# Tiles of the large products allocated on multiples of 256 bytes in a two-block fp32 transformer kernel

## The chip, the cores and the metric

The kernel runs on one core of a Trainium2 chip. The metric is the time of one execution in device microseconds (us). TensorE (PE) multiplies, VectorE (DVE), ScalarE (ACT) and GpSimd (POOL) do the rest, SyncE (SP) issues the transfers from HBM. In one product a *moving* operand streams through the array while a *stationary* operand sits in it; the stationary operand is loaded by a separate operation, which the profile lists as the engine PEld.

## The reference, cut to what matters

Two transformer blocks in a row on 256 tokens of 2048 features, all in fp32:

```
x   = x + norm(mixer(norm(x)) @ w_out)             # three branches: two attentions and an RWKV recurrence
x   = x + norm(square(relu(norm(x) @ w_mlp_up)) @ w_mlp_down)        # 8192 wide
x   = x + concat(pool, latent attention, memory attention) @ w_o
x   = x + (silu(conv(n @ w_gate)) * (n @ w_up)) @ w_down             # 5632 wide, n = norm(x)
```

Nearly all the arithmetic is in the products with the weight matrices: `w_in` (2048 x 12580, with the three gates), `w_out`, `w_mlp_up`, `w_mlp_down`, `w_gate`, `w_up`, `w_down` and smaller ones. The attentions, the recurrence and the norms are small beside them.

## The kernel before, in words

**A number in two parts.** TensorE works on the type fp32r. To keep fp32 accuracy each factor is held as a sum of two fp32r tiles, `hi` and `lo`; a product is `hi*hi + hi*lo + lo*hi`, added up in PSUM. Activations are split once (`split`), into tiles of shape [128, k, 2, 256]: for each slice k of 128 features 256 columns of the high part and then 256 of the low part. Their names in the trace are `uhl` (input of block 1), `yaT`, `ybT`, `ychl` (branches), `mhl` (the mix), `memhl` (memory), `A` (input of the MLP, then of block 2), `B` (hidden layer of the MLP, a group at a time), `kvhl`, `qhl` (latents), `catT`, `x3hl` (input of the last layers) and `h2`, shown as `h` (its hidden layer).

**A unit of weights.** `load` brings 512 KB of weights as [128, 1024] fp32 into `raw` (three buffers) with one transfer issued by SP, ACT copies it to `hi` (three buffers), and DVE writes `lo = raw - hi` (three buffers). All nine buffers are 4096 bytes long in each partition.

**Two kinds of product.** `lin_t` gives the result feature-major: the weights are stationary (128 columns at a time) and the activations move. For every slice of weights it does a *pair*: `hi` against 512 moving columns (both parts of the activations) and `lo` against 256 (the high part). `lin_n` gives the result token-major: the activations are stationary and the weights move, 512 columns at a time (384 for `w_q_up`, 320 for one piece of block 2's `w_in`), three matmuls for a slice: activations high on `hi`, high on `lo`, low on `hi`. So in the trace `m<-uhl,hi` names the moving tile first in `lin_t`, and `m<-hi,B` names the moving weights first and the stationary tile `B` second in `lin_n`. `m` is the PSUM bank; `s` stands for the banks of all small products.

**Order.** A scheduler orders the instructions at build time, and pools decide each tile's address. The splits in `load` have a raised priority, so a unit's `hi` and `lo` are made as soon as its buffers are free. Where a tile asks for nothing, the pools put it on the next multiple of 32 bytes. Every matmul of both kinds goes through the helper at L159, every ACT instruction through L178, every DVE `tensor_tensor` through L166.

**Order of the work in time.** The mixer (`uhl` moving, with the attentions and the recurrence between) to about 890 us, `w_out` (`mhl`) to 981, half of the memory product (`memhl`), four groups of the MLP (`A` moving, then `B` stationary) to 1723, the other half of the memory product, block 2's input product (`A` stationary) to 1836, its attentions to about 1890, `w_o` (`catT`), then three groups of `x3hl` moving and `h` stationary to the end.

Of the kernel before, what the change touches and what calls it, by code (L numbers as in the profile page):

```python
# [10 lines left out]
F32 = mybir.dt.float32  # L11
F32R = mybir.dt.float32r
# [3 lines left out]
PSUM = bass.MemoryType.PSUM  # L16
# [15 lines left out]
NB = 16  # L32

# [90 lines left out]
class K:  # L124
# [78 lines left out]
    def split(self, hl, src, scale=None):  # L203
        """hl: [128, 2, n] F32R; src fp32 (SBUF or PSUM); hl[0] + hl[1] == src * scale."""
        hi, lo = hl[:, 0], hl[:, 1]
        if scale is None:
            self.act(hi, src, AF.Copy)
            self.tt(lo, src, hi.bitcast(F32), ALU.subtract)
        else:
            self.act(hi, src, AF.Identity, scale=scale)  # L210
            self.stt(lo, src, scale, hi.bitcast(F32), ALU.mult, ALU.subtract)

    def load(self, parts, kt, nc_):
        """parts: (column, DRAM rows [kt*128, n]); the weights of one unit, split."""
# [71 lines left out]
    def halves(self, out, ps, m=P, lo=0):  # L286
        """out = the sum of a bank's halves."""
# [4 lines left out]
    def bcast_rows(self, r):  # L292
        """r [128 tok, 2] -> PSUM [128, 256] with r along the free axis on all partitions."""
# [5 lines left out]
    def sum_features(self, acc):  # L299
        """acc [128 feat, 256] -> PSUM [128 tok, 2] of sums over the partitions."""  # L300
# [33 lines left out]
    # decay and in-context rate  # L334
# [11 lines left out]
    # 1 / max(|kk|, 1e-12) by token, chunk and head  # L346
# [20 lines left out]
def rwkv_pair(k, tl, j, zr, zk, zv, sg, aa, rin, omka, col, gu1, gu2, sg1, sg2, yc):  # L367
    """Two heads (128 features); two chunks of 128 tokens."""
    C = k.C
    # features of the recurrence  # L370
# [40 lines left out]
    # token-major copies  # L411
# [12 lines left out]
    # scores, [s, t]; i = 2 * chunk + head  # L424
# [11 lines left out]
    # inverse of I + L: its transpose's blocks of 16 on the diagonal by substitution, each row by itself  # L436
    # (the block's entries, from DRAM, on all of its rows)
# [25 lines left out]
    # doubling of the blocks, here of 16: only every other n columns change  # L463
# [32 lines left out]
    # right-hand sides, solution, outputs, state  # L496
# [36 lines left out]
    # bonus and gate  # L533
# [10 lines left out]
    def finish():  # L544
        # norm by head, gain
# [52 lines left out]
def softmax_tile(k, tl, z, n, p, first=True):  # L598
    """p = softmax over the free axis of z [128, n]."""
# [44 lines left out]
def causal_out(k, tl, z, v, out):  # L644
    """z [128, 384]: scores of queries 0..127 (128 keys) and 128..255 (256 keys)."""
# [14 lines left out]
def mixer(k, a, xhl):  # L660
    """-> mg: mix * norm_mix_post, feature-major, and its factor by token."""
# [38 lines left out]
    yaT = tl([P, 4, 2, 256], "yaT", F32R)  # L700
    ybT = tl([P, 4, 2, 256], "ybT", F32R)
# [54 lines left out]
    # gates and branches  # L756
# [47 lines left out]
def post_stats(k, pool, acc, z, j, n):  # L804
    """acc += z * z (feature-major)."""
# [9 lines left out]
def block_kernel(ctx, tc, vecs, rows, cst1, cst2, out, **a):  # L815
# [19 lines left out]
    xhl = tl(up, [P, 16, 2, 256], "uhl", F32R)  # L835
# [27 lines left out]
    # residual stream, feature-major  # L863
# [4 lines left out]
    # memory: normed and transposed; its keys and values fill the turns between phases  # L868
# [6 lines left out]
    memhl = tl(memp, [P, 16, 2, 256], "memhl", F32R)  # L875
# [67 lines left out]
    # MLP  # L943
# [4 lines left out]
    for g in range(G):  # L948
        h = tl(pB, [P, KG, 2, 256], "B", F32R)
# [24 lines left out]
    def r_mlp(r, ss, t):  # L974
        # y carries no 1/rms of its input yet: y_true = r1^2 y
# [7 lines left out]
    x2hl = tl(pA, [P, 16, 2, 256], "A", F32R)  # L983
# [7 lines left out]
def block2(k, main, pA, a, rows, cst2, x2hl, rz, xres, mk, mv, out):  # L991
# [10 lines left out]
    # projections of the normed input  # L1002
# [40 lines left out]
    def unit_heads(nm_, z):  # L1043
        """The memory attention's queries and keys, over their norms by head."""
# [26 lines left out]
    kvhl = lp.tile([P, 2, 2, 256], F32R, tag="kvhl", name="kvhl")  # L1071
    qhl = lp.tile([P, 4, 2, 256], F32R, tag="qhl", name="qhl")
# [12 lines left out]
    catT = pA.tile([P, 16, 2, 256], F32R, tag="A", name="catT")  # L1085
    # pooling
# [16 lines left out]
    # memory attention  # L1103
# [25 lines left out]
    # keys and values  # L1129
# [19 lines left out]
    # queries; their factors by token join the scores  # L1149
# [18 lines left out]
    # latent attention by pairs of heads  # L1168
# [27 lines left out]
    # output product; x3 and its norm  # L1196
# [11 lines left out]
    x3hl = pB.tile([P, 16, 2, 256], F32R, tag="B", name="x3hl")  # L1208
# [16 lines left out]
    # token-major residual  # L1225
# [11 lines left out]
    for gi, (n0, nn) in enumerate(groups):  # L1237
        h = pA.tile([P, 16, 2, 256], F32R, tag="A", name=k.nm("h2"))
# [73 lines left out]
```

## Time and profile before

| | us |
|---|---|
| runs | 2766.87, 2770.70, 2780.21 (median 2770.7) |
| span of the profiled execution | 2761.2 |
| PE busy | 2691.8 (97%) |
| PEld busy | 2261.6 (82%) |
| DVE busy | 1735.1 (63%) |
| ACT busy | 1391.4 (50%) |
| DMA engines, by their packets | 54% of the span |

The span runs from the first to the last instruction of the program in one profiled execution; a run's time also holds what lies around it. The median run is 9.5 us longer than this span, and the runs themselves lie 13 us apart. The profiled execution's own time is not listed apart from its span. A busy PE is not a PE at its peak: a matmul's row in the trace counts from its start to the modelled end of its last column, and rows overlap, so how fast matmuls follow one another is read from the distance between their starts.

### The profile page before, as it was taken

The numbers are of one execution on the slowest core, as the hardware profiler recorded it, in microseconds if no ns is written. First come the engines' busy times: TensorE is split into PE (matmuls) and PEld (weight loads), VectorE is DVE, ScalarE is ACT, GpSimd is POOL, SyncE is SP. The second block draws the span as 40 slices with busy tenths as digits, with TensorE's granted clock in tenths as the row PEclk, the third lists the DMA queues.
The fourth block names the chain that finished last, engine by engine and source line by source line (L and its number), as shares of the span: only waits on it lengthen the run. The fifth ranks groups of instructions, "written<-read, shape, count | busy, mean of one in ns | idle before, by whom it ended". The sixth has DMA issues, their size and how long they took to land.

```text
span 2761.2 us, 38434 instructions
## 1 busy us (share of the span) xinstructions
PE 2691.8 (97%) x14588; PEld 2261.6 (82%) x14588; DVE 1735.1 (63%) x2985; ACT 1391.4 (50%) x2245; POOL 37.1 (1%) x36
## 2 busy tenths in 40 slices
PE   7999999999999999999999999999999999999999
PEld 6777787877888888888888888878788888888887
DVE  6657576567666566455565565757767567647764
ACT  7445364454555665444344444666655445535543
POOL 0000000000000000000000000000000000000000
PEclk9999999999999999999999999999999999999999
DMA  6444344454456756565565655544456556555555
GB/s 186 131 133 140 109 133 130 147 156 130 151 185 211 257 171 189 187 190 190 189 190 187 189 191 189 173 154 135 136 164 189 188 186 190 185 189 188 186 189 177
DMA packets 390232, 475.69 MB, mean 172 GB/s; under 512 B 20112, under 2 KB 306832, under 8 KB 390048
## 3 DMA queue, kind: packets, MB, share of 16 engines
q1 hardware_dynamic: 390016, 473.18, 54.2%
q8 instruction: 114, 1.87, 0.3%
q14 instruction: 70, 0.57, 0.1%
q0 software_dynamic: 32, 0.07, 0.0%
HBM read 470.82 MB, written 2.36 MB: 171 GB/s over the span
## 4 chain that ended last, share of the span: by engine, by line
PE 83%; issue 5%; DVE 5%; DMA 3%; ACT 1%; POOL 0%; POOLq 0%; SPq 0%; DVEq 0%; ACTq 0%
PE m L159 77%; PE s L159 5%; DMA mb<-md 3%; DVE lo L166 2%; PE s L163 1%; DVE zw L166 1%; DVE zc L166 1%; ACT hi L178 1%; DVE SM L166 0%; DVE Z L166 0%; POOL rs L195 0%; DVE zz L166 0%; DMA raw<-in_w_in 0%; DVE xres L169 0%; POOL qrs L195 0%
## 5 line engine op out<-in xcount | busy, mean ns | idle before, releaser
L166 DVE TENSOR_TENSOR lo<-raw,hi 128x1024 fp32r<-128x1024 f32 (+1 forms) x874 | 1063.2, 1217 | 768.6 <-ACT hi L178 765.2
L178 ACT ACTIVATE hi<-raw 128x1024 fp32r<-128x1024 f32 (+1 forms) x874 | 920.1, 1053 | 1051.3 <-PE m L159 799.5
L159 PE MATMUL m<-uhl,hi 128*128 128x512 f32 (+1 forms) x1456 | 528.7, 403 | 2.4 <-DVE zz L166 2.4
L159 PE MATMUL m<-x3hl,hi 128*128 128x512 f32 x1408 | 494.6, 394 | 0.0
L159 PE MATMUL m<-uhl,lo 128*128 128x256 f32 (+1 forms) x1456 | 419.2, 288 | 13.5 <-DVE lo L166 13.5
L159 PE MATMUL m<-x3hl,lo 128*128 128x256 f32 x1408 | 398.3, 283 | 0.0
L159 PE MATMUL m<-A,hi 128*128 128x512 f32 x1024 | 356.0, 393 | 1.8 <-DVE A L169 1.8
L159 PEld LDWEIGHTS m<-uhl,hi 128*128 128x128 f32 (+1 forms) x1456 | 275.6, 189 | 67.0 <-DVE zz L166 3.3
L159 PE MATMUL m<-hi,B 128*128 128x512 f32 x1024 | 321.6, 395 | 0.0
L159 PEld LDWEIGHTS m<-x3hl,hi 128*128 128x128 f32 x1408 | 264.4, 188 | 61.0
L159 PEld LDWEIGHTS m<-uhl,lo 128*128 128x128 f32 (+1 forms) x1456 | 277.1, 190 | 17.6 <-DVE lo L166 15.2
L159 PE MATMUL m<-A,lo 128*128 128x256 f32 x1024 | 286.7, 281 | 0.0
L159 PEld LDWEIGHTS m<-x3hl,lo 128*128 128x128 f32 x1408 | 264.7, 188 | 0.1
L159 PEld LDWEIGHTS m<-hi,B 128*128 128x128 f32 x1024 | 192.9, 188 | 45.0
L159 PEld LDWEIGHTS m<-A,hi 128*128 128x128 f32 x1024 | 191.8, 188 | 44.8 <-DVE A L169 2.4
L159 PE MATMUL m<-hi,h 128*128 128x512 f32 x704 | 221.7, 395 | 0.0
L159 PE MATMUL m<-lo,B 128*128 128x512 f32 x512 | 202.0, 395 | 0.0
L159 PEld LDWEIGHTS m<-A,lo 128*128 128x128 f32 x1024 | 192.5, 188 | 0.8 <-DVE lo L166 0.3
L159 PEld LDWEIGHTS m<-hi,h 128*128 128x128 f32 x704 | 131.9, 187 | 32.4
L178 ACT ACTIVATE hv<-m 128x256 f32<-128x256 f32 x323 | 120.0, 374 | 55.1 <-PE m L159 53.5
L159 PE MATMUL m<-lo,h 128*128 128x512 f32 x352 | 139.1, 395 | 0.0
L166 DVE TENSOR_TENSOR zz<-m,hv 128x256 f32<-128x256 f32 x307 | 126.9, 418 | 17.7 <-ACT hv L178 17.7
(373 smaller groups left out, 3014.6 us busy)
## 6 DMA issues: line engine op xcount, KB each, us to landing
raw<-in_w_in SPq DMA_DIRECT2D x220, 512.0 KB, 3.5
raw<-in_w_mlp_up SPq DMA_DIRECT2D x128, 512.0 KB, 3.8
raw<-in_w_mlp_down SPq DMA_DIRECT2D x128, 512.0 KB, 3.4
raw<-in_w_gate SPq DMA_DIRECT2D x88, 512.0 KB, 3.5
raw<-in_w_up SPq DMA_DIRECT2D x88, 512.0 KB, 3.6
raw<-in_w_down SPq DMA_DIRECT2D x88, 512.0 KB, 3.5
raw<-in_w_out SPq DMA_DIRECT2D x32, 512.0 KB, 4.6
raw<-in_w_o SPq DMA_DIRECT2D x32, 512.0 KB, 3.6
```

What stands on the lines that cost most here:

```text
L159: self.pe.matmul(out, lhsT=lhsT, rhs=rhs, start=start, stop=stop)
L163: self.pe.transpose(out, in_, self.C["ident"][:n, :n])
L166: self.v.tensor_tensor(out=out, in0=a, in1=b, op=op)
L178: self.a.activation(out, in_, f, **k)
```

## The change

Seventeen allocations ask for a start on a multiple of 256 bytes: the three tiles of `load` (`raw`, `hi`, `lo`, three buffers each) and all split activations. Nothing else is changed in the program text but that comments are blank lines now, and that the new constant moves each later line down by one (L159 is L160 in the changed kernel).

```diff
 NB = 16
+LINE = 256
@@ load
-        raw = self.wr.tile([P, 1024], F32, tag="raw", name=self.nm("raw"))
-        hi = self.wh.tile([P, 1024], F32R, tag="hi", name=self.nm("hi"))
-        lo = self.wl.tile([P, 1024], F32R, tag="lo", name=self.nm("lo"))
+        raw = self.wr.tile([P, 1024], F32, tag="raw", name=self.nm("raw"), align_bytes=LINE)
+        hi = self.wh.tile([P, 1024], F32R, tag="hi", name=self.nm("hi"), align_bytes=LINE)
+        lo = self.wl.tile([P, 1024], F32R, tag="lo", name=self.nm("lo"), align_bytes=LINE)
@@ block_kernel
-    xhl = tl(up, [P, 16, 2, 256], "uhl", F32R)
+    xhl = tl(up, [P, 16, 2, 256], "uhl", F32R, align_bytes=LINE)
...
-        h = tl(pB, [P, KG, 2, 256], "B", F32R)
+        h = tl(pB, [P, KG, 2, 256], "B", F32R, align_bytes=LINE)
...
-    x3hl = pB.tile([P, 16, 2, 256], F32R, tag="B", name="x3hl")
+    x3hl = pB.tile([P, 16, 2, 256], F32R, tag="B", name="x3hl", align_bytes=LINE)
```

Likewise `yaT`, `ybT`, `mhl`, `ychl`, `memhl`, the three tiles in the place `A` (`act_hl`, `x2hl`, `catT`), `kvhl`, `qhl` and `h2`. The addresses that the pools give in the two built programs, as bytes in a partition (the three buffers of a kind lie 4096 bytes apart, so the first stands for all):

| tile | before | rest by 256 | rest by 64 | changed | rest by 256 |
|---|---|---|---|---|---|
| raw | 24672 | 96 | 32 | 24832 | 0 |
| hi | 36960 | 96 | 32 | 37376 | 0 |
| lo | 49248 | 96 | 32 | 49920 | 0 |
| uhl | 67936 | 96 | 32 | 68608 | 0 |
| A, catT, h2 | 97088 | 64 | 0 | 97792 | 0 |
| yaT, ybT | 113120, 121312 | 224 | 32 | 114176, 122624 | 0 |
| memhl | 129856 | 64 | 0 | 130816 | 0 |
| kvhl, qhl | 177056, 181152 | 160 | 32 | 178176, 182272 | 0 |
| ychl | 180192 | 224 | 32 | 179968 | 0 |
| mhl, B, x3hl | 196576 | 224 | 32 | 196352 | 0 |

Within these tiles a matmul's operand starts at a multiple of 512 bytes from the tile's start in all cases but two: the weights of the 36 columns of the decay and forget gates (144 bytes a slice), and the moving weights of 320 columns (1280 bytes a slice).

No instruction changes its place on any engine. As tiles lie at other addresses, other old tiles lie under them, and three ACT instructions change what they wait for. Two are in this stretch of ACT's order, at the split of the memory and the first output of `w_out` (`memhl` and `tok`; `hi_...<-raw_...` are the splits of the weights). Before:

```order
755 L178 ACTIVATE memhl_8874<-mt_9495,Vall 128x256 [waits DMAHW7_49,DVE_49]
756 L178 ACTIVATE memhl_8874<-mt_9495,Vall 128x256
757 L178 ACTIVATE hi_9009<-raw_9008 128x1024 [waits DMAHW6_49,DVE_49,PE_49]
758 L178 ACTIVATE memhl_8874<-mt_9495,Vall 128x256 x2
759 L178 ACTIVATE memhl_8874<-mt_9505,Vall 128x256 [waits DMAHW1_49]
760 L178 ACTIVATE hi_9035<-raw_9034 128x1024 [waits DMAHW0_49,DVE_49,PE_49]
761 L178 ACTIVATE memhl_8874<-mt_9505,Vall 128x256 x3
762 L178 ACTIVATE hi_9053<-raw_9052 128x1024 [waits DMAHW2_49,DVE_49,PE_49]
763 L178 ACTIVATE tok_8878<-m_8880 128x512 [waits PE_49]
```

The same stretch of ACT's order in the changed kernel:

```order
755 L179 ACTIVATE memhl_8874<-mt_9495,Vall 128x256 [waits DMAHW7_49,DVE_49,Pool_49]
756 L179 ACTIVATE memhl_8874<-mt_9495,Vall 128x256
757 L179 ACTIVATE hi_9009<-raw_9008 128x1024 [waits DMAHW6_49,DVE_49,PE_49]
758 L179 ACTIVATE memhl_8874<-mt_9495,Vall 128x256 x2
759 L179 ACTIVATE memhl_8874<-mt_9505,Vall 128x256 [waits DMAHW1_49]
760 L179 ACTIVATE hi_9035<-raw_9034 128x1024 [waits DMAHW0_49,DVE_49,PE_49]
761 L179 ACTIVATE memhl_8874<-mt_9505,Vall 128x256 x3
762 L179 ACTIVATE hi_9053<-raw_9052 128x1024 [waits DMAHW2_49,DVE_49,PE_49]
763 L179 ACTIVATE tok_8878<-m_8880 128x512 [waits PE_49,Pool_49]
```

Rows 755 and 763 wait for an earlier POOL instruction as well; the third, the first split into `mhl`, loses such a wait.

## Rows read from the trace of the kernel before

**Rows 1.** From the page: the span, the busy time of the engines, PE's slices, the granted clock, and the chain of work that ended last, by engine and by line.

```profile
span 2761.2 us, 38434 instructions
PE 2691.8 (97%) x14588; PEld 2261.6 (82%) x14588; DVE 1735.1 (63%) x2985; ACT 1391.4 (50%) x2245; POOL 37.1 (1%) x36
...
PE   7999999999999999999999999999999999999999
...
PEclk9999999999999999999999999999999999999999
...
PE 83%; issue 5%; DVE 5%; DMA 3%; ACT 1%; POOL 0%; POOLq 0%; SPq 0%; DVEq 0%; ACTq 0%
PE m L159 77%; PE s L159 5%; DMA mb<-md 3%; DVE lo L166 2%; PE s L163 1%; DVE zw L166 1%; DVE zc L166 1%; ACT hi L178 1%; DVE SM L166 0%; DVE Z L166 0%; POOL rs L195 0%; DVE zz L166 0%; DMA raw<-in_w_in 0%; DVE xres L169 0%; POOL qrs L195 0%
```

**Rows 2.** The groups of PE by line, tile and shape: how many there are, us busy, mean ns of one, idle time before them. The moving tile stands first among the inputs in `lin_t`, `hi` first in `lin_n`, where the groups that move `lo` hold half as many matmuls and are left out.

```profile
L159 PE MATMUL m<-uhl,hi 128*128 128x512 f32 x1440 | 523.2, 403 | 2.4 <-DVE zz L166 2.4
L159 PE MATMUL m<-x3hl,hi 128*128 128x512 f32 x1408 | 494.6, 394 | 0.0
L159 PE MATMUL m<-A,hi 128*128 128x512 f32 x1024 | 356.0, 393 | 1.8 <-DVE A L169 1.8
L159 PE MATMUL m<-hi,B 128*128 128x512 f32 x1024 | 321.6, 395 | 0.0
L159 PE MATMUL m<-hi,h 128*128 128x512 f32 x704 | 221.7, 395 | 0.0
...
L159 PE MATMUL m<-hi,mhl 128*128 128x512 f32 x256 | 80.4, 395 | 0.0
L159 PE MATMUL m<-hi,A 128*128 128x512 f32 x192 | 61.1, 396 | 0.0
...
L159 PE MATMUL m<-ychl,hi 128*128 128x512 f32 x128 | 45.3, 393 | 0.0
L159 PE MATMUL m<-hi,memhl 128*128 128x512 f32 x128 | 40.5, 395 | 0.0
...
```

**Rows 3.** PE's instructions on one tile in one undisturbed stretch: count, shortest/median/longest ns of one, first and last start in us. `A` and `x3hl` are moving tiles of `lin_t`; the three below are moving weights of `lin_n`, where every third matmul moves `lo`.

```profile
L159 PE MATMUL m<-A,hi x256: 392/392/397, 1189.2 to 1277.6; 128*128 128x512 f32 x128
L159 PE MATMUL m<-x3hl,hi x512: 387/396/400, 2218.1 to 2397.5; 128*128 128x512 f32 x171
...
L159 PE MATMUL m<-lo,B x128: 390/393/404, 1278.2 to 1366.7; 128*128 128x512 f32 x128
L159 PE MATMUL m<-lo,h x128: 393/396/398, 2398.1 to 2487.0; 128*128 128x512 f32 x128
L159 PE MATMUL m<-lo,memhl x32: 393/395/397, 981.7 to 1003.4; 128*128 128x512 f32 x32
```

**Rows 4.** PE in order of time (start us, us of the row, what): first and last rows of four stretches with no stall in them. From the first to the last start there are 32 pairs of `uhl`; 31 pairs and one matmul of 512 of `uhl`; 15 matmuls of `lin_n` with `uhl` stationary; 9 matmuls of `lin_n` of 384 columns with `qhl` stationary.

```profile
136.79 0.39 PE L159 MATMUL m<-uhl,hi 128*128 128x512 f32 x1
...
147.88 0.39 PE L159 MATMUL m<-uhl,hi 128*128 128x512 f32 x1
...
757.00 0.40 PE L159 MATMUL m<-uhl,hi 128*128 128x512 f32 x1
...
768.19 0.28 PE L159 MATMUL m<-uhl,lo 128*128 128x256 f32 x1
...
186.59 0.39 PE L159 MATMUL m<-lo,uhl 128*128 128x512 f32 x1
...
189.99 0.39 PE L159 MATMUL m<-lo,uhl 128*128 128x512 f32 x1
...
1859.35 0.34 PE L159 MATMUL m<-lo,qhl 128*128 128x384 f32 x1
...
1860.91 0.34 PE L159 MATMUL m<-lo,qhl 128*128 128x384 f32 x1
```

**Rows 5.** Pairs of `uhl` behind a long wait: PE's busy time, the granted clock and the DMA share in the stretch, then two starts of `hi` one pair apart in it, in order of time.

```profile
620.40:623.40 3.00, 3.00 (x11) 0.50 0.72 214
...
621.00 0.63 PE L159 MATMUL m<-uhl,hi 128*128 128x512 f32 x1
...
621.64 0.63 PE L159 MATMUL m<-uhl,hi 128*128 128x512 f32 x1
```

**Rows 6.** All engines in a stretch of mixed products (`x3hl`, then `h`) and in two of `lin_n` (`B`, `mhl`): length, then PE, PEld, DVE, ACT and POOL busy us (with counts), granted clock, DMA share and GB/s.

```profile
2200.00:2400.00 200.00, 200.00 (x1113) 173.79 (x1112) 142.36 (x232) 103.55 (x150) 0.00 (x0) 1.00 0.59 188
1280.00:1367.00 87.00, 87.00 (x376) 70.52 (x376) 43.46 (x43) 33.20 (x32) 0.00 (x0) 1.00 0.55 189
892.50:981.40 88.90, 88.90 (x384) 72.10 (x383) 48.46 (x57) 52.54 (x80) 0.70 (x1) 1.00 0.72 253
```

**Rows 7.** The longest pieces of the chain of work that ended last, of the second half (start us, us, what), and POOL's instruction before the memory's split with that split's own row (count, ns, first and last start us).

```profile
712.03 292.03 PE m L159 x1504
1016.25 22.86 PE m L159 x129
1039.60 706.13 PE m L159 x3517
...
2025.33 731.62 PE m L159 x3820
...
709.97 1.05 POOL L195 TENSOR_TENSOR rs<-rp,mhalf 128x4 f32<-128x4 f32 x1 [52.83 <-DVE rp L175]
...
L178 ACT ACTIVATE memhl<-mt,Vall x16: 490/500/511, 906.3 to 922.2; 128x256 fp32r<-128x256 f32 x16
```

More of the change, by code (lines that the diff above doesn't have):

```diff
@@ L699, in mixer @@
     yc = tl([P, 8, 256], "yc")
-    yaT = tl([P, 4, 2, 256], "yaT", F32R)
-    ybT = tl([P, 4, 2, 256], "ybT", F32R)
+    yaT = tl([P, 4, 2, 256], "yaT", F32R, align_bytes=LINE)
+    ybT = tl([P, 4, 2, 256], "ybT", F32R, align_bytes=LINE)
     rst, ast = ExitStack(), ExitStack()
@@ L792, in mixer @@
     hp = k.phase(k.rightctx, "mh", side="right")
-    mhl = hp.tile([P, 16, 2, 256], F32R, tag="mhl", name="mhl")
+    mhl = hp.tile([P, 16, 2, 256], F32R, tag="mhl", name="mhl", align_bytes=LINE)
     yst = ExitStack()
     yp = k.phase(yst, "yc", side="right")
-    ychl = yp.tile([P, 8, 2, 256], F32R, tag="ychl", name="ychl")
+    ychl = yp.tile([P, 8, 2, 256], F32R, tag="ychl", name="ychl", align_bytes=LINE)
     for j in range(8):
@@ L874, in block_kernel @@
     memp = k.phase(mst, "mem")
-    memhl = tl(memp, [P, 16, 2, 256], "memhl", F32R)
+    memhl = tl(memp, [P, 16, 2, 256], "memhl", F32R, align_bytes=LINE)
     ml = k.phase(mst, "mlp")
@@ L912, in block_kernel @@
     pB = k.phase(rst, "pB", side="right")
-    act_hl = tl(pA, [P, 16, 2, 256], "A", F32R)
+    act_hl = tl(pA, [P, 16, 2, 256], "A", F32R, align_bytes=LINE)
     def add_norm(z, ss4, r_of, gain, hl, gain2):
@@ L982, in block_kernel @@
     mem_product(1)
-    x2hl = tl(pA, [P, 16, 2, 256], "A", F32R)
+    x2hl = tl(pA, [P, 16, 2, 256], "A", F32R, align_bytes=LINE)
     r2 = add_norm(y, ss4, r_mlp, "norm_mlp_post", x2hl, "g_mix_2")
@@ L1070, in block2 @@
     k.lin_n(w2, x2hl, KD, [(1024, 320), (512, 512)], ev_z)
-    kvhl = lp.tile([P, 2, 2, 256], F32R, tag="kvhl", name="kvhl")
-    qhl = lp.tile([P, 4, 2, 256], F32R, tag="qhl", name="qhl")
+    kvhl = lp.tile([P, 2, 2, 256], F32R, tag="kvhl", name="kvhl", align_bytes=LINE)
+    qhl = lp.tile([P, 4, 2, 256], F32R, tag="qhl", name="qhl", align_bytes=LINE)
     lat(zkv, 256, "g_kv_lat_2", kvhl)
@@ L1083, in block2 @@
     k.lin_n(w2, x2hl, KD, [(1344, 512), (0, 512)], ev_z)
-    catT = pA.tile([P, 16, 2, 256], F32R, tag="A", name="catT")
+    catT = pA.tile([P, 16, 2, 256], F32R, tag="A", name="catT", align_bytes=LINE)
     band = lp.tile([P, 1536], F32, tag="zq", name="band")
@@ L1237, in block2 @@
     for gi, (n0, nn) in enumerate(groups):
-        h = pA.tile([P, 16, 2, 256], F32R, tag="A", name=k.nm("h2"))
+        h = pA.tile([P, 16, 2, 256], F32R, tag="A", name=k.nm("h2"), align_bytes=LINE)
         for n in range(n0, n0 + nn):
```

## Prediction

> **What bounds the kernel now.** Read the share of the engines and the chain of waits first [rows 1]: PE is busy for 97% of the span, 83% of the chain is PE, and 77% is one line of it, the matmuls of the large products. From 712 us to the end the chain is almost nothing but `PE m` pieces, four of them 1,753 us long together [rows 7]. In such stretches DVE and ACT are busy for 38 to 71% of the time, the DMA engines for 55 to 72%, PE for all of it [rows 6]. The granted clock is full there, 2.4 GHz. So what counts is how fast one matmul follows another, and that is read from starts, not from rows: a row of 512 columns shows 387 to 404 ns in every group [rows 2, 3], because rows overlap.
>
> From the starts: a pair of `lin_t` (512 and 256 columns) with `A` moving takes (1277.6 - 1189.2)/255 = 346.7 ns; with `x3hl` (2397.5 - 2218.1)/511 = 351.1 ns [rows 3]. With `uhl` there are two speeds: (147.88 - 136.79)/32 = 346.6 ns in one stretch, and (768.19 - 757.00 - 0.235)/31 = 353.4 ns in another, the 0.235 being the one matmul of 512 over, taken a little above the fastest [rows 4]. A matmul of `lin_n` of 512 columns takes, as a third of the distance of two `lo`, 232.3 ns with `B` stationary, 233.3 with `h`, 233.3 with `memhl` [rows 3], but (189.99 - 186.59)/15 = 226.7 ns with `uhl` [rows 4]. At 384 columns it is (1860.91 - 1859.35)/9 = 173.3 ns [rows 4]. The same code, the same clock, operands that differ in address alone: so address does seem to matter, by 1 to 3%.
>
> All the fast cases have one form: columns/2.4 GHz + 13.3 ns (213.3 + 13.3 = 226.7; 160 + 13.3 = 173.3; a pair 320 + 26.7 = 346.7). I call this the floor. The slow cases lie 4.4 to 6.7 ns over it. Set beside the table of rests by 256: `lin_n` is on the floor where moving and stationary tile have the same rest (`hi` 96, `uhl` 96), and off it where they differ (96 against 224 or 64). `lin_t` is on the floor always with `A` (64 against 96) in the quoted stretch, sometimes with `uhl` (96 against 96), never in the quoted stretch of `x3hl` (224 against 96, half of 256 apart).
>
> **The change part by part.** No instruction moves or goes. All rests by 256 become 0, so all moving and stationary tiles have the same one.
> - *`lin_n`.* I take it that the same rest puts all of them where `uhl` is now. `B` and `mhl`: 1,536 + 384 matmuls (half as many again as the rows of `hi` [rows 2]) times 5.6 ns (232.3 - 226.7; for `mhl` 88.9 us/384 = 231.5 agrees to its rounding [rows 6]) = 10.8 us. `h`, `memhl` and `A` of 512 columns: 1,056 + 192 + 288 times 6.6 ns = 10.1 us. Together 20.9 us. The stretch with `uhl` and those of 384 columns gain nothing.
> - *`lin_t`.* `x3hl` loses its rest half of 256 away: 1,408 pairs times 4.4 ns (351.1 - 346.7) = 6.2 us. The 128 pairs of `ychl` [rows 2], with the same rest, give 0.6 us more. `A`'s 1,024 pairs are on the floor and stay. `uhl` I leave as it is, half on the floor and half off it. Together 6.8 us.
> - *Bounds.* If the same rest sets `lin_t` into the slow pair of `uhl`, `x3hl` pays 2.3 ns more instead (3.2 us) and `A` 6.7 ns (1,024 pairs, 6.9 us): `lin_t` then costs 10.1 us. If `uhl` goes to the floor for good, at most 1,440 times 6.7 = 9.6 us come on top. Between these ends I take the 6.8, on the better side, since `A` stayed on the floor for 255 pairs on end.
> - *The two new waits on POOL* cost nothing: POOL's instruction before them ends at 711 us, and the first split of the memory, which now waits for it, starts at 906.3 [rows 7]; the first output of `w_out` comes later still.
> - *`raw` on a multiple of 256* touches only DMA, ACT and DVE. Their work hides under PE [rows 6]: if the transfers got no faster, nothing is lost, and if they did, nothing is gained where PE is the bound. PE uses a unit up in 8 pairs, 2.81 us at 351.1 ns; at 346.7 it is 2.77, so no cover is used up.
>
> The sum: 20.9 + 6.8 = 28 us, nearly all of it in stretches where the chain is PE alone. The span goes from 2761.2 to about 2733. The median of the runs stands 9.5 us over that span, so the run goes from 2770.7 to 2742 us. The likeliest case's own range runs from 2733 (`uhl` on the floor too) to 2760 (`lin_t` pays 10.1, `lin_n` gives 20.9).
>
> **The rivals.**
> - *The address was not what made the difference.* `uhl` shows two speeds at one and the same address [rows 4], so some state carried over from stall to stall chooses between them, and the changed kernel would draw new lots with the same mean. Against it: `x3hl` and `B` keep their speeds over 511 pairs and 381 matmuls. Time: 2770, within 0.5% (14 us, about what a measurement of this kernel can tell from no change). [...]
> - *The floor itself falls.* No moving tile before starts at rest 0 or 128, so the 13.3 ns over the columns' own time may itself be the price of a start off the line. For it: behind a wait, at a granted clock of 0.50 (1.2 GHz), a pair takes 621.64 - 621.00 = 0.640 us, just 768 columns at that clock [rows 5], so the extra is not work of the array but something that hides when the array is slow. Against it: it is the same at rests of 64 and 96, and at 384 and 512 columns, as a fixed gap would be. Price: some 11,500 matmuls (the groups of [rows 2], those of `lin_t` twice, those of `lin_n` one and a half times) times 13.3 ns = 153 us beside 37 (the 28 and `uhl`'s 9.6): 2581 us if all of it goes, about 2657 if half does. [...]
> - *Slower: the same rest is the bad case.* In `lin_t` the slowest pair of all, 353.4 ns, has moving and stationary tile at the same rest. If that is the cause and `uhl`'s 226.7 in `lin_n` comes from elsewhere, all pairs go to 353.4: 10.1 us for `x3hl` and `A`, 0.3 for `ychl`, and, if half of `uhl`'s pairs are fast now, 720 times 6.7 ns = 4.8, with nothing gained in `lin_n`: 2786 us. It decides from the point where `lin_n` gives less than 1 us of its 21; at 15 both cancel.
>
> **How the numbers follow.** Likeliest case 0.48, of which 0.02 ends above 2757; no effect 0.20; the floor falls 0.20; slower 0.12. Faster by over 0.5%: 0.46 + 0.20 = 0.66; within: 0.22; slower: 0.12. The predicted time is the likeliest case's, 2742 us. To leave out no more than 2 in 10 the range must take in nearly all of "no effect" (up to 2778) and the lesser half of "the floor falls" (from 2650): 0.48 + 0.19 + 0.13 = 0.80.
>
> **What would show it.** In the changed kernel's trace: two `lo` of `lin_n` 680 ns apart with `B`, `h`, `mhl` and `memhl` (now 697 to 700); pairs of `x3hl` at 346.7 (now 351.1) and of `A` still at 346.7; counts, waits of DVE and ACT and the granted clock as before. Pairs near 320 to 335 show the second rival, pairs at 353 under `A` the third. I am wrong at the root if `B` and `x3hl` keep 232.3 and 351.1.

## The result, and the profile after

The changed kernel takes 2750.6 us in the median of 5 runs (2748.05 to 2755.87) beside 2770.7 for the kernel before (5 runs, 2763.42 to 2780.21). The ratio of the runs is 0.9939, interval [0.9916, 0.9961], so 0.4 to 0.8% faster; the two medians alone give 0.9927. The prediction said 2742 us. The changed kernel's profiled span is 2748.4 us, 12.8 less than before [rows 1]. A run is 2.1 to 2.2 us longer than its span, here and in every later run, so the 9.5 us between span and median of the kernel before were no fixed cost: a span of 2761.2 us belongs to a run of about 2763.4, the fastest of its five.

From the page of the changed kernel: the span, the engines' busy time, the granted clock, the chain of work that ended last (L160 is L159 of before).

```profile
span 2748.4 us, 38434 instructions
PE 2682.7 (98%) x14588; PEld 2261.9 (82%) x14588; DVE 1734.2 (63%) x2985; ACT 1390.1 (51%) x2245; POOL 37.1 (1%) x36
PEclk9999999999999999999999999999999999999999
PE 81%; issue 5%; DVE 5%; DMA 3%; ACT 1%; POOL 0%; SPq 0%; POOLq 0%; DVEq 0%; ACTq 0%
```

Counts, DVE, ACT and clock are as before; PE alone lost busy time, 9.1 us. So the pace of the matmuls is where to look. The rows that answer to [rows 3], of the same stretches of the changed kernel:

```profile
L160 PE MATMUL m<-A,hi x256: 389/398/403, 1183.2 to 1273.3; 128*128 128x512 f32 x128
L160 PE MATMUL m<-x3hl,hi x512: 389/398/403, 2208.0 to 2388.6; 128*128 128x512 f32 x171
L160 PE MATMUL m<-lo,B x128: 389/389/398, 1273.8 to 1360.2; 128*128 128x512 f32 x128
L160 PE MATMUL m<-lo,h x128: 387/389/398, 2389.2 to 2475.6; 128*128 128x512 f32 x128
L160 PE MATMUL m<-lo,memhl x32: 389/389/389, 977.6 to 998.6; 128*128 128x512 f32 x32
```

`lin_n` went to the floor: (1360.2 - 1273.8)/381 = 226.8 ns with `B` (232.3 before) and as much with `h` (233.3). `lin_t` went the other way: a pair with `A` takes (1273.3 - 1183.2)/255 = 353.3 ns (346.7 before), with `x3hl` (2388.6 - 2208.0)/511 = 353.4 (351.1 before). `uhl` got better in its last 170 us, where [rows 4] had 353.4 ns:

```profile
L160 PE MATMUL m<-uhl,hi x32: 392/394/395, 756.2 to 766.9; 128*128 128x512 f32 x32
```

(766.9 - 756.2)/31 is 345.2 by rounded ends, with 346.6 by the unrounded starts: a fast stretch. The last 352 pairs of `uhl` are all slow before and all fast here, 6.5 ns a pair or 2.3 us in all.

A smaller loss stands in one place of the chain of waits. From 880 to 1004 us the kernel before shows one unbroken piece of PE; the changed kernel's chain passes through the transfers of the memory there. First the row of before, then three of after (start us, us, what), then what waited in the changed kernel from 925 to 945 us (us in all, times, longest).

```profile
879.99 124.07 PE m L159 x551
```

```profile
927.98 6.81 DMA mt<-in_mem
...
938.07 1.24 DVE lo L167
939.35 59.91 PE m L160 x263
```

```profile
ACT mt L179 <- DMA mt<-in_mem: 4.4, 3, 3.5
PEld m L160 <- DVE lo L167: 1.2, 2, 0.7
PE m L160 <- DVE lo L167: 0.3, 1, 0.3
```

ACT waited for `mt`, the weights' copies queued behind it, and PE waited for their `lo`, about a microsecond in all. That the faster `lin_n` brings this on is not shown: the same wait of PE's loads for `lo` is there, 0.7 us, in a kernel below whose `lin_n` has its old pace (`lin_t` alone), and it is missing in another with `lin_n` on the floor (`lin_n` alone).

### The profile page after: what moved, and what is told of

The parts are those of the page before. It is cut to its first block, busy times and chain, and to the rows that moved or that the text cites. A ratio compares the mean times of both kernels' runs of the same rounds, so it can differ in the third digit from the quotient of the medians.

```text
span 2748.4 us, 38434 instructions
## 1 busy us (share of the span) xinstructions
PE 2682.7 (98%) x14588; PEld 2261.9 (82%) x14588; DVE 1734.2 (63%) x2985; ACT 1390.1 (51%) x2245; POOL 37.1 (1%) x36
## 4 chain that ended last, share of the span: by engine, by line
PE 81%; issue 5%; DVE 5%; DMA 3%; ACT 1%; POOL 0%; SPq 0%; POOLq 0%; DVEq 0%; ACTq 0%
PE m L160 75%; PE s L160 5%; DMA mb<-md 2%; DVE lo L167 2%; PE s L164 1%; ACT hi L179 1%; DVE zw L167 1%; DVE zc L167 1%; DMA mt<-in_mem 0%; DMA mt<-in_memT 0%; DVE SM L167 0%; DVE Z L167 0%; POOL rs L196 0%; DVE zz L167 0%; DMA raw<-in_w_in 0%
## 5 line engine op out<-in xcount | busy, mean ns | idle before, releaser
L167 DVE TENSOR_TENSOR lo<-raw,hi 128x1024 fp32r<-128x1024 f32 (+1 forms) x874 | 1062.8, 1217 | 757.8 <-ACT hi L179 754.5
L160 PE MATMUL m<-uhl,hi 128*128 128x512 f32 (+1 forms) x1456 | 528.4, 403 | 2.4 <-DVE zz L167 2.4
L160 PE MATMUL m<-x3hl,hi 128*128 128x512 f32 x1408 | 497.8, 399 | 0.0
L160 PE MATMUL m<-uhl,lo 128*128 128x256 f32 (+1 forms) x1456 | 419.2, 288 | 13.5 <-DVE lo L167 13.5
L160 PE MATMUL m<-x3hl,lo 128*128 128x256 f32 x1408 | 395.5, 281 | 0.0
L160 PE MATMUL m<-A,hi 128*128 128x512 f32 x1024 | 362.0, 399 | 1.8 <-DVE A L170 1.8
L160 PEld LDWEIGHTS m<-uhl,hi 128*128 128x128 f32 (+1 forms) x1456 | 277.0, 190 | 65.8 <-DVE zz L167 3.4
L160 PEld LDWEIGHTS m<-x3hl,hi 128*128 128x128 f32 x1408 | 264.6, 188 | 66.1
L160 PE MATMUL m<-hi,B 128*128 128x512 f32 x1024 | 315.9, 389 | 0.0
L160 PEld LDWEIGHTS m<-uhl,lo 128*128 128x128 f32 (+1 forms) x1456 | 277.8, 191 | 17.5 <-DVE lo L167 15.1
L160 PE MATMUL m<-A,lo 128*128 128x256 f32 x1024 | 287.3, 281 | 0.0
L160 PEld LDWEIGHTS m<-x3hl,lo 128*128 128x128 f32 x1408 | 266.0, 189 | 0.1
L160 PEld LDWEIGHTS m<-A,hi 128*128 128x128 f32 x1024 | 192.0, 188 | 49.2 <-DVE A L170 2.4
L160 PEld LDWEIGHTS m<-hi,B 128*128 128x128 f32 x1024 | 192.2, 188 | 40.0
L160 PE MATMUL m<-hi,h 128*128 128x512 f32 x704 | 217.4, 389 | 0.0
L160 PE MATMUL m<-lo,B 128*128 128x512 f32 x512 | 199.2, 389 | 0.0
L160 PEld LDWEIGHTS m<-A,lo 128*128 128x128 f32 x1024 | 193.3, 189 | 0.8 <-DVE lo L167 0.2
L160 PEld LDWEIGHTS m<-hi,h 128*128 128x128 f32 x704 | 132.1, 188 | 27.6
L160 PE MATMUL m<-lo,h 128*128 128x512 f32 x352 | 137.0, 389 | 0.0
```

Of the source, the lines that this page charges most:

```text
L160: self.pe.matmul(out, lhsT=lhsT, rhs=rhs, start=start, stop=stop)
L167: self.v.tensor_tensor(out=out, in0=a, in1=b, op=op)
```

## The experiments

Below, the *distance* is start of the moving tile minus start of the stationary one for `lin_t`, stationary minus moving for `lin_n` (activations minus weights in both), by 256. Theory 1: the distance sets the pace, not the address. Where a kernel below gives a tile a place of its own, it does so through one helper that cuts the tile out of a slightly longer one; nothing but places differs:

```diff
+def at(pool, kk, tag, name, off):
+    t = pool.tile([P, kk * 512 + 64], F32R, tag=tag, name=name, align_bytes=LINE)
+    return t[:, off // 4 : off // 4 + kk * 512].rearrange("p (k a t) -> p k a t", a=2, t=256)
```

**Equal, but on no multiple of 256.** Built on the kernel before, where `hi`, `lo` and `uhl` start at 96 as they are; `B`, `x2hl`, `mhl`, `memhl`, `catT`, `x3hl`, `h2`, `kvhl` and `qhl` are placed as `A` is here.

```diff
-    act_hl = tl(pA, [P, 16, 2, 256], "A", F32R)
+    act_hl = at(pA, 16, "A", k.nm("A"), 96)
```

> Every moving and stationary tile of the large products, weights included, starts 96 bytes past a multiple of 256 (yaT, ybT and ychl, 5% of the pairs, elsewhere): all starts are equal by 256, as in the changed kernel, but none lies on a multiple of 256. Nothing of the computation is left out. Theory 1 (what counts is the distance by 256 between the starts of the moving and the stationary tile): lin_n on its floor of 226.7 ns with all tiles as in the changed kernel, pairs of lin_t at one of the two speeds 346.7 or 353.3 ns, and the time within 8 us of the changed kernel's 2750.6 us. Rival (the start itself must lie on a multiple of 256): lin_n back at 232 to 233 ns, the time at 2768 to 2772 us, that of the kernel before.

Measured: 2749.96 us (2746.7 to 2751.67), ratio 0.9945 [0.993, 0.996]. Its rows: `B`, then two stretches of `A` and two of `x3hl`.

```profile
L165 PE MATMUL m<-lo,B x128: 389/389/397, 1274.8 to 1361.2; 128*128 128x512 f32 x128
...
L165 PE MATMUL m<-A,hi x174: 392/394/400, 1036.7 to 1096.7; 128*128 128x512 f32 x174
L165 PE MATMUL m<-A,hi x256: 389/398/404, 1184.1 to 1274.2; 128*128 128x512 f32 x128
...
L165 PE MATMUL m<-x3hl,lo x358: 274/279/280, 2015.0 to 2138.8; 128*128 128x256 f32 x179
...
L165 PE MATMUL m<-x3hl,hi x512: 389/398/404, 2204.2 to 2384.7; 128*128 128x512 f32 x171
```

`lin_n` takes 86.4/381 = 226.8 ns with no tile on a multiple of 256: the multiple is not needed, equality is (the other seven distances, in the table below, have 228.9 to 234.4). And `lin_t` has two paces in one run at one distance: `A` 60.0/173 = 346.8, then 90.1/255 = 353.3; `x3hl` 123.8/357 = 346.8, then 180.5/511 = 353.2.

**Other distances.** The changed kernel with its weights left on multiples of 256 and the activations at various starts: besides the two tiles shown, `x3hl` at 32, `uhl` 128, `ychl` 64, `catT` 192, `x2hl` (shown as `A` in `lin_n`) 32, `memhl` 64, `mhl` 96, `h2` 192.

```diff
-    act_hl = tl(pA, [P, 16, 2, 256], "A", F32R, align_bytes=LINE)
+    act_hl = at(pA, 16, "A", k.nm("A"), 224)
-        h = tl(pB, [P, KG, 2, 256], "B", F32R, align_bytes=LINE)
+        h = at(pB, KG, "B", k.nm("B"), 128)
```

> Weights start on multiples of 256; each activation tile starts at another distance from one: in lin_n the stationary tile is at 32 (x2hl), 64 (memhl), 96 (mhl), 128 (B), 192 (h2) and 128 (uhl); in lin_t the moving tile is at 224 (A), 32 (x3hl), 128 (uhl), 64 (ychl), 192 (catT). Nothing of the computation is left out. Theory 1 (the distance counts): lin_n at 232.4 ns with B and uhl, which was 226.7 for uhl in both kernels so far, and 231 to 234 ns with all others but kvhl and qhl; lin_t with A at 346.7 ns a pair (distance of A in the kernel before), uhl at 351.1 all the time (distance of x3hl before), with none of its two speeds; x3hl unknown, between 346.7 and 353.3. Rival (it is enough that the weights start on a multiple of 256): lin_n at 226.7 ns with all tiles, and the time that of the changed kernel. One look: 2765 to 2775 us by theory 1, 2750 by the rival.

Measured: 2754.16 us in one run.

```profile
L165 PE MATMUL m<-lo,B x128: 390/393/404, 1280.8 to 1369.3; 128*128 128x512 f32 x128
...
L165 PE MATMUL m<-lo,h x128: 388/388/397, 2394.5 to 2481.7; 128*128 128x512 f32 x128
...
L165 PE MATMUL m<-lo,mhl x128: 392/397/400, 893.2 to 982.5; 128*128 128x512 f32 x128
...
L165 PE MATMUL m<-lo,memhl x32: 392/396/398, 983.2 to 1004.9; 128*128 128x512 f32 x32
...
L165 PE MATMUL m<-lo,A x58: 392/396/403, 1798.1 to 1838.0; 128*128 128x512 f32 x58
...
L165 PE MATMUL m<-x3hl,hi x512: 390/390/397, 2216.8 to 2393.9; 128*128 128x512 f32 x171
...
L165 PE MATMUL m<-catT,lo x88: 279/281/282, 1980.2 to 2010.9; 128*128 128x256 f32 x88
```

Weights on a multiple alone do not put `lin_n` on its floor of 226.8: `B` at 128 takes 88.5/381 = 232.3 ns, `mhl` at 96 234.4, `memhl` at 64 and `A` at 32 233.3; `h` at 192 gave 228.9, outside what I expected, and `A` at 224 had 353.2 ns in its first long stretch and 346.7 in the other three, where I expected 346.7 alone. The time lies below the 2765 to 2775 us expected, near the rival's 2750, but not for the rival's reason, since `lin_n` is off the floor: against the kernel before, `x3hl` at 32 gives 1,408 times 4.4 ns, 6.2 us, and `h` at 192 1,056 times 4.4, 4.6 us. The find is `x3hl` at 32: 177.1/511 = 346.6 ns, in all three of its stretches.

**Split places.** Weights and `lin_n`'s stationary tiles on multiples, the tiles that `lin_t` moves 32 bytes ahead of one, where `A` was fast in [rows 3]; `x3hl`, `uhl`, `catT`, `ychl`, `yaT` and `ybT` are placed as `A` is here.

```diff
-    act_hl = tl(pA, [P, 16, 2, 256], "A", F32R, align_bytes=LINE)
+    act_hl = at(pA, 16, "A", k.nm("A"), 224)
```

> The changed kernel, but the tiles that lin_t moves (A of the first block, x3hl, uhl, catT, ychl, yaT, ybT) start 32 bytes ahead of a multiple of 256; weights and all stationary tiles of lin_n stay on one, except uhl, which is both. Nothing of the computation is left out. Theory 1: lin_n stays at 226.7 ns (but for uhl, 192 matmuls, 233), A, x3hl, catT and uhl run at 346.7 ns a pair as A did in the kernel before, and against the changed kernel A and x3hl give 1,024 times 6.6 and 1,408 times 6.6 ns, 16 us, catT 1.5 us: 2730 to 2738 us. Rival (the slow pair of lin_t is drawn by chance at each stall, whatever the distance): A or x3hl at 353.3 in parts, and a time within 8 us of 2750.6.

Measured: 2745.16 us (2739.98 to 2751.92), ratio 0.9937 [0.9918, 0.9957], above the 2730 to 2738 us expected. Two stretches of `A`, then two of `x3hl`:

```profile
L165 PE MATMUL m<-A,hi x174: 392/394/402, 1037.6 to 1098.7; 128*128 128x512 f32 x174
L165 PE MATMUL m<-A,hi x256: 392/392/397, 1186.1 to 1274.5; 128*128 128x512 f32 x128
...
L165 PE MATMUL m<-x3hl,lo x358: 279/280/283, 2012.7 to 2138.8; 128*128 128x256 f32 x179
...
L165 PE MATMUL m<-x3hl,hi x512: 392/392/397, 2204.3 to 2381.4; 128*128 128x512 f32 x171
```

353.2 and 346.7 ns for `A`, 353.2 and 346.6 for `x3hl`: this distance has two paces as well. The rival was right in that; that the pace falls by chance whatever the distance is not shown, and the placement 32 bytes behind, below, speaks against it.

**The raw tile free.**

```diff
-        raw = self.wr.tile([P, 1024], F32, tag="raw", name=self.nm("raw"), align_bytes=LINE)
+        raw = self.wr.tile([P, 1024], F32, tag="raw", name=self.nm("raw"))
```

> The changed kernel without the alignment of the raw weights: their tile starts where the allocator puts it, all else stays on multiples of 256. Nothing of the computation is left out. Theory 1 (the raw tile plays no part): 2748 to 2756 us, lin_n at 226.7 ns, splits by DVE and ACT as long as before (1,217 ns for a lo of 1,024 columns). Rival (the raw tile's place gives part of the gain through faster splits or transfers): over 2757 us, and longer splits.

Measured: 2753.06 us in one run; a `lo` of 1,024 columns takes 1,217 ns in both kernels. `lin_n` is at 226.7 ns as in the changed kernel. No part of the gain was seen to come from `raw`.

**32 bytes behind.** The same as the split placement, with 32 in place of 224 for the same seven tiles.

```diff
-    act_hl = tl(pA, [P, 16, 2, 256], "A", F32R, align_bytes=LINE)
+    act_hl = at(pA, 16, "A", k.nm("A"), 32)
```

> As the split placement, but the tiles that lin_t moves (A of the first block, x3hl, uhl, catT, ychl, yaT, ybT) start 32 bytes behind a multiple of 256, where x3hl showed 346.7 ns in all three of its stretches; weights and all stationary tiles of lin_n on a multiple, except uhl, which is both. Nothing of the computation is left out. Theory 1, with this distance as one that has only the fast pair: A, x3hl, catT and uhl at 346.7 ns throughout, lin_n at 226.7 (uhl 233). Against the changed kernel A gives 1,024 times 6.3, x3hl 1,408 times 6.6, uhl 1,440 times 2.3, catT 256 times 4.5 ns, and the 192 matmuls with uhl stationary cost 1.2 us: 19 us in all, 2730 to 2734 us, 0.986 to 0.988 of the kernel before. Rival (x3hl drew the fast pair three times by chance): A or uhl show 353.3 in parts, 2738 to 2748 us.

Measured: 2732.37 us (2730.13 to 2735.86), ratio 0.986 [0.9839, 0.988].

```profile
L165 PE MATMUL m<-lo,B x128: 389/389/395, 1268.7 to 1355.1; 128*128 128x512 f32 x128
...
L165 PE MATMUL m<-A,hi x174: 390/390/396, 1032.4 to 1092.3; 128*128 128x512 f32 x174
L165 PE MATMUL m<-A,hi x256: 390/390/399, 1179.7 to 1268.2; 128*128 128x512 f32 x128
...
L165 PE MATMUL m<-x3hl,hi x512: 390/390/399, 2195.0 to 2372.2; 128*128 128x512 f32 x171
...
L165 PE MATMUL m<-uhl,hi x32: 390/390/390, 753.6 to 764.3; 128*128 128x512 f32 x32
```

`A` takes 346.2 and 347.1, `x3hl` 346.8 ns: no slow stretch is left, and rows of one kind are nearly all of one length. This is faster than both kernels. Once more:

> The kernel with lin_t's moving tiles 32 bytes behind the rest of the weights and lin_n's stationary tiles at the same rest, once more. Nothing of the computation is left out. Theory 1 (this distance has one speed alone): every stretch of A, x3hl, uhl and catT again at 346.7 ns a pair, B, h2, mhl and memhl at 226.7, 2728 to 2736 us. Rival (its fast stretches were drawn): any stretch of over 90 pairs at 353.3.

Measured: 2728.56 us in one run; `A` again 60.0/173 = 346.8 in the stretch that was slow in the changed kernel:

```profile
L165 PE MATMUL m<-A,hi x174: 390/390/394, 1030.6 to 1090.6; 128*128 128x512 f32 x174
L165 PE MATMUL m<-x3hl,hi x512: 390/390/399, 2192.9 to 2370.1; 128*128 128x512 f32 x171
```

**One part alone, and the other.** Both are built on the kernel before. In the first `mhl`, `memhl`, `B`, `x2hl` and `h2` are set to the rest of the weights (96), and `A`, `catT` (64) and `x3hl` (224) held at their old rests.

```diff
-        h = tl(pB, [P, KG, 2, 256], "B", F32R)
+        h = at(pB, KG, "B", k.nm("B"), 96)
```

> The kernel before with one part of the change: the stationary tiles of lin_n (mhl, memhl, B, x2hl, h2) start 96 bytes past a multiple of 256, as the weights do there; A, x3hl, catT and all other tiles of lin_t keep the places that they have in the kernel before. Nothing of the computation is left out. Theory 1: lin_n at 226.7 ns, lin_t as before (A 346.7, x3hl 351.1, uhl mixed), 20 to 22 us under the kernel before, ratio 0.992 to 0.9935, and so a little faster than the changed kernel, since lin_t doesn't pay. Rival (the gain of the changed kernel is partly that of lin_t or of the weights' place): a ratio of 0.995 or more.

In the second `A`, `catT` and `x3hl` are set to 96, and `lin_n`'s tiles held at their old rests (`B` and `mhl` 224, the others 64).

```diff
-    act_hl = tl(pA, [P, 16, 2, 256], "A", F32R)
+    act_hl = at(pA, 16, "A", k.nm("A"), 96)
```

> The kernel before with the other part of the change: A, catT and x3hl, which lin_t moves, start 96 bytes past a multiple of 256, as the weights do there; the stationary tiles of lin_n keep the rests that they have in the kernel before (224 and 64). Nothing of the computation is left out. Theory 1: lin_n at 232.4 and 233.3 ns as before, A and x3hl at either 346.7 or 353.3 ns in each stretch, so between -9 us (all fast) and +10 us (all slow) of the kernel before; ratio 0.997 to 1.004. Rival of the prediction (the same rest puts lin_t on its floor): -6 us, ratio 0.998, with x3hl and A at 346.7 in every stretch.

Measured: `lin_n` alone 2743.85 us (2738.96 to 2745.94), ratio 0.9897 [0.9877, 0.9918], better than expected, and each run of it faster than each of six runs of the whole change on the same chip (2747.45 to 2758.16); `lin_t` alone 2769.15 us (2762.37 to 2773.93, 10 runs), ratio 0.9998 [0.9982, 1.0014]. So `lin_n` gave all of the gain. By spans `lin_n` alone gives 2761.2 - 2741.4 = 19.8 us; the larger figures of the runs (24.2 between the medians, 1.03% of 2768 or 28.5 by the ratio) have in them that the kernel before was profiled in its fastest execution. Both parts' own rivals are dead: `lin_n` alone is not at 0.995 or more, and in `lin_t` alone `A` and `x3hl` are not at 346.7 in every stretch. In the second of the two, the four long stretches of `A` at one address have 353.2, 346.7, 353.3 and 346.7 ns. `B`, at its old distance of 128, takes 88.9/381 = 233.3 ns in its first stretch there (last row), where it had 232.3 so far: this distance has two paces too.

```profile
L165 PE MATMUL m<-A,hi x174: 393/398/403, 1043.2 to 1104.3; 128*128 128x512 f32 x174
L165 PE MATMUL m<-A,hi x256: 390/391/397, 1194.2 to 1282.6; 128*128 128x512 f32 x128
L165 PE MATMUL m<-A,hi x256: 389/398/403, 1372.2 to 1462.3; 128*128 128x512 f32 x128
L165 PE MATMUL m<-A,hi x256: 389/391/396, 1551.9 to 1640.3; 128*128 128x512 f32 x128
...
L165 PE MATMUL m<-lo,B x128: 392/395/398, 1104.9 to 1193.8; 128*128 128x512 f32 x128
```

**The changed kernel and the kernel before once more.**

> The changed kernel once more, beside the others. Nothing of the computation is left out. Theory 1 with two speeds of lin_t drawn by the state in which a stretch is entered: lin_n at 226.7 ns as in its first profile, A after B again at 353.3 in the second, third and fourth group if the entry is the same each time, x3hl and uhl free to differ from the first profile; ratio 0.992 to 0.996. Rival (the speeds of lin_t belong to the addresses alone): every stretch of A, x3hl and uhl at the speed of the first profile within 0.5 ns.

> The kernel before once more. Nothing of the computation is left out. Theory 1: lin_n at 232.4 and 233.3 ns as in its first profile; A and uhl, whose distance has two speeds (moving tile 32 ahead of the stationary one, and the same), may draw others per stretch, x3hl (half of 256 away) stays at 351.1; each stretch of A that turns slow costs 256 times 6.6 = 1.7 us, so the span may lie up to 7 us above 2761.2. Rival (the speeds belong to the addresses alone): each stretch of A and uhl within 0.5 ns of its first profile, and a span that differs for other reasons.

Measured: the changed kernel 2752.53 us (2747.45 to 2758.16), ratio 0.9931 [0.9913, 0.9949]; the kernel before 2759.09 us in one run. The long stretches of `A` and `x3hl` of the changed kernel came out as in its first profile; `uhl` did not. First `uhl` in the changed kernel's second profile, then one stretch of `A` in the first and the second profile of the kernel before:

```profile
L160 PE MATMUL m<-uhl,hi x32: 395/398/403, 756.4 to 767.4; 128*128 128x512 f32 x32
```

```profile
L159 PE MATMUL m<-A,hi x174: 392/392/392, 1039.7 to 1099.6; 128*128 128x512 f32 x174
```

```profile
L159 PE MATMUL m<-A,hi x174: 389/397/402, 1035.9 to 1097.0; 128*128 128x512 f32 x174
```

`uhl` has rows of 398 ns where it had 394, and 11.0/31 = 354.8 ns a pair by rounded ends (353.6 by the unrounded starts); `A` takes 59.9/173 = 346.2 and then 61.1/173 = 353.2. The same program, the same addresses, another pace: where a distance has two paces, the addresses alone do not choose between them. One execution shows it too. The first profile of the kernel before has both paces of `A`: behind a stall, 40 pairs from the first to the second of these starts take (1038.71 - 1024.58)/40 = 353.3 ns, a microsecond ahead of the fast stretch just shown.

```profile
1024.58 0.40 PE L159 MATMUL m<-A,hi 128*128 128x512 f32 x1
...
1038.71 0.40 PE L159 MATMUL m<-A,hi 128*128 128x512 f32 x1
```

**The remaining distances.** As the other sweep; besides the two tiles shown, `x3hl` at 160, `uhl` 32, `catT` 96, `ychl` 192, `h2` 224, `mhl` 192, `memhl` 96, `x2hl` 128. Two runs of one kernel.

```diff
-    act_hl = tl(pA, [P, 16, 2, 256], "A", F32R, align_bytes=LINE)
+    act_hl = at(pA, 16, "A", k.nm("A"), 64)
-        h = tl(pB, [P, KG, 2, 256], "B", F32R, align_bytes=LINE)
+        h = at(pB, KG, "B", k.nm("B"), 160)
```

> A second set of distances, weights on multiples of 256: in lin_t the moving tile is 64 (A), 160 (x3hl, yaT, ybT), 32 (uhl), 96 (catT) and 192 (ychl) bytes past one; in lin_n the stationary tile 160 (B), 224 (h2), 192 (mhl), 96 (memhl), 128 (x2hl) and 32 (uhl). Nothing of the computation is left out. Theory 1 (the distance sets the speed, whichever tile has it): the same distances give what they gave before with other tiles: uhl 346.7 ns a pair without slow parts (as x3hl at 32), A at 353.3 (as the short ychl at 64), h2 233.3 (distance of h2 in the kernel before), mhl 228.9 (as h2 at 192), memhl 234.3 (as mhl at 96), x2hl 232.4 or 233.3 (as B at 128); x3hl and B at 160 unknown, between floor and the slowest seen. Rival (tiles differ by something other than the distance, their pool or what runs beside them): A stays near 347, or uhl stays mixed with a mean of 349 to 352.

> The second set of distances once more, since its first execution had a granted clock of 0.56 throughout: in lin_t the moving tile is 64 (A), 160 (x3hl, yaT, ybT), 32 (uhl), 96 (catT) and 192 (ychl) bytes past the rest of the weights; in lin_n the stationary tile 160 (B), 224 (h2), 192 (mhl), 96 (memhl), 128 (x2hl) and 32 (uhl). Nothing of the computation is left out. Theory 1: uhl at 346.7 ns a pair without slow parts, A at 353.3, h2 233.3, mhl 228.9, memhl 234.3, x2hl 232.4 or 233.3; x3hl and B at 160 unknown, between floor and the slowest seen; 2755 to 2775 us at a full clock. Rival (tiles differ by something other than the distance): A near 347, or uhl mixed. If the clock is low again, the kernel's addresses bear on the clock; if it is full, the low clock was the chip's.

Measured: 4378.85 us in the first run, at a granted clock of 0.556 in the mean (0.54 to 0.56 from 60 us on); 2758.03 us in the second, on another chip, at 0.99. So these addresses do not by themselves bring that clock about. What did is open: on the first chip the kernel before ran beside it at 0.99 (2769.28 and 2759.09 us). The second run's rows:

```profile
L165 PE MATMUL m<-lo,B x128: 394/394/394, 1274.5 to 1363.4; 128*128 128x512 f32 x128
...
L165 PE MATMUL m<-lo,memhl x32: 392/397/400, 975.7 to 997.5; 128*128 128x512 f32 x32
...
L165 PE MATMUL m<-x3hl,lo x512: 277/280/284, 2217.5 to 2394.7; 128*128 128x256 f32 x171
...
L165 PE MATMUL m<-A,hi x174: 392/392/396, 1033.6 to 1093.9; 128*128 128x512 f32 x174
L165 PE MATMUL m<-A,hi x256: 388/397/398, 1183.8 to 1273.9; 128*128 128x512 f32 x128
...
L165 PE MATMUL m<-hi,mhl x111: 392/394/397, 937.4 to 975.2; 128*128 128x512 f32 x111
...
L165 PE MATMUL m<-catT,lo x88: 278/279/282, 1978.3 to 2008.7; 128*128 128x256 f32 x88
```

The same distance gave the same pace under another tile: `memhl` at 96 21.8/93 = 234.4 ns (`mhl` had 234.4), `mhl` at 192 37.8/165 = 229.1 (`h` had 228.9; 110 steps of `hi` are 165 matmuls). One expectation failed: `A` at 64 had 60.3/173, about 349 ns, in its first stretch and 353.3 only after it. All distances together, in ns, from the rows shown here and in [rows 3]:

| distance by 256 | 0 | 32 | 64 | 96 | 128 | 160 | 192 | 224 |
|---|---|---|---|---|---|---|---|---|
| `lin_n`, one matmul | 226.8 | 233.3 | 233.3 | 234.4 | 232.3 or 233.3 | 233.3 | 228.9 | 233.3 |
| `lin_t`, one pair | 346.7 or 353.3 | 346.7 | 349 or 353.3 | 349.4 | 351.1 | 346.8 | 352.9 | 346.7 or 353.2 |

## Why the prediction was right or wrong, point by point

- *Address sets the pace, clock and counts stay.* Right. The rival that address makes no difference is dead: moving `lin_n`'s tiles alone gave 0.8 to 1.2%. Its ground was sound all the same: at the distances of 0 and 224 `lin_t` has two paces at one and the same addresses (`A` 346.7 and 353.3 ns at 0, in `lin_t` alone; 346.2 and 353.2 at 224, in two executions of the kernel before).
- *`lin_n` to the floor, 20.9 us.* Right in mechanism and size. With the paces found the sum is 1,536 + 384 matmuls times 5.6 and 1,056 + 192 + 288 times 6.5, 20.7 us; `lin_n` alone gave 19.8 by spans.
- *`lin_t` -6.8 us.* This is the step that failed: "`x3hl` loses its rest half of 256 away" and goes to 346.7, and "`A`'s 1,024 pairs are on the floor and stay". I read the fast `A` as a property of its place and took equality to be as good for `lin_t` as for `lin_n`. But equality has two paces, and the changed kernel had the slow one in every stretch of `A` and `x3hl` of over 90 pairs, in both profiles: 1,024 times 6.6 and 1,408 times 2.3 make 10 us lost, the very bound of 10.1 that I worked out and passed over. I argued "since `A` stayed on the floor for 255 pairs on end", and length proves nothing: in each long stretch of `A` and `x3hl` in the profiles before and after, the pace of its start lasts to its end (quarter by quarter `A` has 346.7 ns before and 353.0 to 353.5 after, `x3hl` 351.0 to 351.1 and 353.2 to 353.4). The trace before me had `A` at 353.3 ns as well, up to 1038.7 us, and I didn't read that stretch. I also left `uhl` as "half on the floor and half off it"; in that trace about a quarter of its undisturbed pairs are on the floor, and none of the last 352. The changed kernel has those on it, 2.3 us that I had at nothing, and in its second profile off it again.
- *The sum.* 20.9 less 10, with `uhl`'s gain of 2.3 us, is what the 12.8 us of the spans and the 15 to 20 of the medians show, in place of 28. That the forecast came within 9 us is `lin_n`'s doing alone. The part of `lin_t` that has two paces and the kernel before's own spread (2760.84 to 2780.63 in one set of 17 runs) leave a few us that I can't divide.
- *The slow end of the likeliest case's own range*, 2760 with `lin_t` paying 10.1, is thus the case that came about; measured from the profiled span (2761.2 - 20.9 + 10.1 = 2750.4) it is within 2 us of the span after.
- *The floor falls.* Dead: tiles on multiples of 256 in both operands stay at 226.8 and, at best, 346.7 ns, so the 13.3 ns a matmul over the columns' own time are there as before. That time is one that the rows give: 226.7 ns for 512 columns and 346.7 for a pair of 768 make (2 times 226.7 - 346.7)/256 = 0.4168 ns a column, 2.4 columns a ns at a granted clock of 1.00 [rows 6]; the 2.4 GHz of the prediction is shown as this rate alone.
- *Slower: equality is the bad case.* Half right: in `lin_t` it can be, in `lin_n` it is the best of the eight distances. Since `lin_n` gave its 21, the kernel got faster.
- *The raw tile and the new waits on POOL cost nothing.* Nothing against it was seen; the kernel with `raw` free ran like the changed one, in one run. The waits on POOL were tested by no run of their own.
- *"No cover is used up".* Nearly right. In the stretch of `mhl` PE waited for `lo` behind a late transfer of the memory, about 1 us; I had looked at `lin_t`'s cover alone. Why it came late is open, for kernels of either pace of `lin_n` have the wait and others of either pace have not.

## What to carry to other kernels

Read the pace of back-to-back matmuls from the distance of their starts, stretch by stretch, and set it against the distance by 256 of the two operands' starts: what paid here was the relation of the two, not a round address, and the two kinds of product wanted different ones (equal where weights move, 226.8 ns against 228.9 to 234.4 at the other distances; activations 32 bytes behind the weights where activations move, 346.7 ns against 346.7 or 353.3 at equality). Before a fast stretch is put down to its address, look whether the same address is slow in another stretch or another execution, as `A` in the kernel before had 346.2 ns in one execution and 353.2 in the next. An alignment that is good for one product and bad for another is best tried on each alone.

## What the runs showed of the hardware that I had not expected

- At one pair of addresses `lin_t` has two steady paces, 346.7 and 353.3 ns, which hold over hundreds of pairs. In part the pace went with what came before the stretch. Counted over the profiles at full clock, long stretches of `A` and `x3hl` that follow `lin_n` without a stall had one pace: all 17 at distance 224 the fast one, and all 20 at distance 0 behind a `lin_n` at 0 the slow one, the changed kernel's among them. So its slow `lin_t` was no bad luck. Behind a `lin_n` off its floor (`lin_t` alone) 2 of 5 stretches at 0 were fast, and behind a stall both paces came at either distance (at 0, 346.8 ns with all tiles at 96 and 353.2 in the changed kernel; at 224, 346.2 and 353.2 in the kernel before). What the two paces come from is not shown by any run here.
- At distance 32 the pair had the fast pace alone: `A`, `x3hl` and `uhl` in the two profiles of that placement, `x3hl` and `uhl` in one more each (345.2 to 347.1 ns by rounded ends). At 160 `x3hl` had 346.8 ns in all its stretches, in one profile.
- At a low clock no cost of the distance was seen, in the one run that had it. In it, at the mean granted clock of 0.556, `B` at 160 took (1699.6 - 1668.5)/81 = 384.0 ns and `mhl` at 192 (1475.5 - 1329.1)/381 = 384.3, where at the full clock they differ by 4.2 (233.3 and 229.1). By the 0.4168 ns a column of the full clock's rows, 512 columns at 0.556 of that clock are 383.8 ns, an estimate as good as that mean clock: next to nothing of the floor's 13.3 ns is left, as in [rows 5], where nothing was. The rows of that run:

```profile
L165 PE MATMUL m<-lo,B x28: 560/562/648, 1668.5 to 1699.6; 128*128 128x512 f32 x28
...
L165 PE MATMUL m<-lo,mhl x128: 559/562/652, 1329.1 to 1475.5; 128*128 128x512 f32 x128
```
